# A macaron decoder layer on eight cores: first input in two transfers, norm additions on pairs of blocks, and an instruction order planned with a new DMA model

## The chip, the cores and the metric

The kernel runs on all 8 cores of one Trainium2 chip, one launch, every core with its own share of the data. The time of a run is the device time of the slowest core in microseconds (us). Cores 0 to 3 lie on one die and cores 4 to 7 on the other; "pairs" below are the cores 0 and 1, 2 and 3, 4 and 5, 6 and 7.

Some executions of any kernel here fall into a slower state, in which one or both dies have a lower granted TensorE clock. Such runs are left out of every comparison: 16 of the runs of the changed kernel and of the experiments, and a few of the kernel before. "Fast runs" are the others.

A ratio of two kernels is the mean time of one kernel's fast runs over the mean of the other's fast runs of the same rounds on the same chip, so it is not quite the ratio of the medians that are quoted beside it. The interval behind it is a 95% interval.

## The reference, cut to what matters

One layer; per token the model width is 1024 and the inner width of a feed-forward part (FFN) is 2816. Each core handles one prompt of 2048 tokens with 16 learned tokens ahead of it, and 16 single-token samples: 2080 tokens.

```python
def _rmsnorm(x, g):
    xf = x.astype(jnp.float32)
    y = xf * lax.rsqrt(jnp.mean(xf * xf, axis=-1, keepdims=True) + EPS) * g.astype(jnp.float32)
    return y.astype(x.dtype)

def _swiglu(x, w_gate, w_up, w_down):
    return (jax.nn.silu(x @ w_gate) * (x @ w_up)) @ w_down

def _layer(x, buf_a, buf_b, h0, p):
    x = x + 0.5 * _rmsnorm(_swiglu(_rmsnorm(x, p['g_ffn1_pre']), ...), p['g_ffn1_post'])
    m, nba, nbb, hl = _mixer(_rmsnorm(x, p['g_mix_pre']), buf_a, buf_b, h0, p)   # conv, RG-LRU, gates
    x = x + _rmsnorm(m, p['g_mix_post'])
    x = x + 0.5 * _rmsnorm(_swiglu(_rmsnorm(x, p['g_ffn2_pre']), ...), p['g_ffn2_post'])
    return x, nba, nbb, hl
```

So there are six norms: three before a part ("pre") and three after it ("post"), and each post norm is followed by an addition to x.

## The kernel before

The 2080 tokens lie on the free axis and are cut into five streams of 414 to 418 columns. The model width lies on the partitions in 8 blocks (KC = 8). Streams 0 and 1 form the first group and share each weight as it arrives in fp32 (`wall`, cast to bf16 on the way). The bf16 copy is written back to a scratch buffer (`wsc`), from which streams 2, 3 and 4 read it again, one after the other. Weights come in units of up to 512 KB through a ring of 10 slots (`wring`). Stream 2 joins early: while streams 0 and 1 work through their first FFN, TensorE can also do stream 2's matmuls, because these wait for nothing that streams 0 and 1 produce. I call such matmuls filler.

```python
SIZES = [418, 418, 416, 414, 414]
GROUPS = [[0, 1], [2], [3], [4]]
NW = 10                       # weight slots
XSTEP = [2, 4, 4, 4, 4]       # blocks of x in one transfer, by stream
HEAD = 4
WARM = (44, 12, 10, 10, 40, 50)   # dummy matmuls, meant to keep TensorE's clock up in the head
LAGS = [...]; STARTS = [...]; ENDS = [...]; CLASSES = {...}   # tuned priorities, cut
```

The program records operations with what they read and write; a list scheduler then fixes the order on every engine before anything runs. It plays the operations through a cost model, always takes the one that can start first, and among those within 0.05 us the one with the best tuned priority. On the chip each engine works in this order. An operation whose input is late holds up everything behind it on that engine, even work that is ready.

```python
CAST_BW = 265e3; COPY_BW = 400e3; INPUT_BW = 320e3     # bytes per us
DMA_CAP = (0.72, 0.95); HW_SHARE = (0.43, 0.22)        # when both DMA queues are busy

    def dma(self, eng, fn, reads, writes, nbytes, cast=False, bw=None):
        ...
        o.xfer = nbytes / (bw or (CAST_BW if cast else COPY_BW))
        o.issue = 0.6 if eng == "pool" else 0.1

    def finalize(self):
        ...
        while remaining:
            for e in self.ENGS:
                ...                       # candidates whose inputs and buffers are there
                lo = min(c[0] for c in cands)
                pick = min((c for c in cands if c[0] <= lo + PRI_EPS), key=lambda c: (c[1], c[2]))
            ...
            order[o.eng].append(o)
```

The head: stream 0's x comes in four transfers, the first weight unit and stream 1's x follow on the other queue once the second of them is there, and ScalarE squares stream 0's blocks.

```python
        def issue_unit(g, u):
            S.dma("pool", lambda e: e.dma_start(out=v[0:n](), in_=rows(src, off, n)),
                  [R_xs(STREAMS[0], 3)] if g == 0 else [("wsc", u)], [v, ("wl", g, u)], ...)

        def rms_finish(ps, n):
            rv = newf()
            act(rv[0:n], ps[0:n], AF.Ln, n, [ps] + DP, [rv], bias=EPS, psum=True)   # DP: derived parameters
            act(rv[0:n], rv[0:n], AF.Exp, n, [rv], [rv], scale=-0.5)
            return rv

        def pre_norm(st, gvi, o, halo):
            if st.i <= 1 and gvi == 0:                 # first norm of streams 0 and 1
                for kc in range(KC):
                    sq = newq()
                    act(sq[0:m], xs_view(st, kc, o, n), AF.Square, m, [R_xs(st, kc)], [sq])
                    if st.i == 0 and kc % 2 == 0:
                        keep_warm(WARM[kc // 2])
                    mm_group(ps[0:m], m, [ones[:, :]], [sq[0:m]], ...)     # sum over partitions
            ...                                         # other norms: squares, VectorE sums, one matmul
            rv = rms_finish(ps, m)

        def post_norm(st, acc, o, src32, src_res):
            rv = rms_finish(acc, m)
            for oc in range(KC):
                tv = newf()
                tt(tv[0:m], src32[s][:, oc, 0:m], rv[0:m], ALU.mult, m, src_res(oc, s) + [rv], [tv])
                tt(xs_view(st, oc, o, n), xs_view(st, oc, o, n), tv[0:m], ALU.add, m, ...)

        first(-999.0, load_x, STREAMS[0], "sp", [])
        head = [first(-998.0, issue_unit, 0, 0)]
        first(-997.0, load_x, STREAMS[1], "pool", [R_xs(STREAMS[0], 3)])
```

`final_norm`, the last post norm, is built like `post_norm` and stores two blocks of the output at a time.

## Time and profile before

| | before |
|---|---|
| time, median of 3 runs | 1564.99 us (1564.85 to 1565.97) |
| profiled execution, slowest core (core 0) | 1563.7 us; the 8 cores 1557.1 to 1563.7 us |
| matmuls on each core | 8771 |
| median step from one matmul's start to the next | 0.176 us |
| after the last matmul, mean of 8 cores | 14.3 us |

The page of the profiled execution, core 0. The first line is the busy time of each engine with its share of the span and the number of instructions, the second the chain of work that ended last, by engine.

```profile
...
PE 1532.3 (98%) x8771; PEld 847.6 (54%) x8771; DVE 813.1 (52%) x1535; ACT 771.8 (49%) x1367; POOL 247.7 (16%) x470
...
PE 93%; DVE 3%; DMA 2%; issue 1%; ACT 1%; DVEq 0%; POOL 0%; SPq 0%; ACTq 0%; POOLq 0%
...
```

TensorE is busy 98% of the span. Other engines' work costs time only where TensorE waits for it, so what has to be read is the waits of TensorE. The list of TensorE's waits, core 0 (what it waited for, then us in total, number of times, longest):

```profile
...
engine line waited for: us in total, times, longest us
PE P L662 <- ACT qp L676: 5.9, 5, 3.1
PE P L662 <- DVE qp L680: 3.9, 2, 2.8
PE P L662 <- DVE xs L704: 2.6, 2, 2.2
...
```

These waits are 17 us in all. They understate the loss: after a wait TensorE's clock can fall to one half for a while. The first columns are the stretch and TensorE's busy time with the number of matmuls; near the end of a line stand the granted clock, the DMA share and GB/s.

```profile
...
core 0: us, PE busy (x) PEld busy (x) DVE busy (x) ACT busy (x) POOL busy (x), PEclk, DMA share, GB/s
30.00:100.00 70.00, 67.17 (x371) 36.39 (x370) 22.57 (x40) 19.09 (x35) 3.43 (x7) 0.98 0.85 211
270.00:340.00 70.00, 68.53 (x387) 37.29 (x386) 63.85 (x116) 54.44 (x104) 7.46 (x14) 1.00 0.77 186
1200.00:1260.00 60.00, 57.79 (x319) 31.25 (x318) 47.70 (x119) 36.58 (x64) 11.04 (x21) 0.97 0.54 177
...
```

A full 70 us holds 398 matmuls of 0.176 us. From 30 to 100 us only 371 started, at a clock of 0.98: that is the wait at 77 us with its half-clock stretch. From 1200 to 1260 us it is 319 of 341 possible, for the same reason. A line of the timeline of TensorE on core 0, with the idle time before the instruction in brackets:

```profile
...
80.22 0.34 PE L662 MATMUL P<-qp,ones 128*128 128x416 bf16 x1 [2.83 <-DVE qp L680]
...
```

At 77 us TensorE stood idle for 2.83 us in front of one matmul of stream 2's first norm (416 columns), behind VectorE's sum of the squares for it.

The stretch from 270 to 340 us lies where streams 0 and 1 pass from FFN 1 to the mixer, with four norms on VectorE and ScalarE. The matmuls between 276 and 300 us on core 0, by shape (stream 0's mixer has 402 to 422 columns here, stream 2 has 416):

```profile
...
L662 PE MATMUL P<-hy,wring 128*128 128x416 bf16 x67 | 12.6, 339 | 0.0
L662 PE MATMUL P<-hy,wring 128*128 128x420 bf16 x32 | 6.4, 340 | 0.4 <-ACT fp L676 0.4
L662 PE MATMUL P<-hy,wring 128*128 128x422 bf16 x16 | 3.2, 342 | 0.0
L662 PE MATMUL P<-hy,wring 128*128 128x402 bf16 x16 | 3.0, 332 | 0.0
...
```

Half of this, 67 matmuls or 11.8 us at 0.176 us each, is stream 2's FFN 1, the filler. Stream 1's norm, which these norms end with, comes late and costs little, the timeline of TensorE says:

```profile
...
304.01 0.34 PE L662 MATMUL P<-qp,ones 128*128 128x418 bf16 x1 [1.06 <-DVE qp L680]
...
```

The tail, groups of VectorE instructions after the last projection, core 0 (shape and count, then busy us and mean ns):

```profile
...
L680 DVE TENSOR_TENSOR big<-xs,fp 128x414 f32<-128x414 f32 x8 | 4.7, 591 | 0.8
L680 DVE TENSOR_TENSOR fp<-hy,fp 128x414 f32<-128x414 f32 x8 | 4.7, 584 | 5.0 <-ACT fp L676 5.0
...
```

Sixteen operations of about 0.59 us each, one after the other, with nothing left for TensorE to do.

### The profile page before, as it was taken

To read this page: it belongs to the slowest core of one execution; us is meant where nothing else is said; L and a number is where in the kernel's file an instruction comes from. 1 tells how busy PE (TensorE), PEld (TensorE's weight loads), DVE (VectorE), ACT (ScalarE), POOL (GpSimd) and SP (SyncE) were. 2 spreads that over 40 slices of the span, in tenths; PEclk is the share of its full clock that TensorE was granted. 3 is DMA by queue.
4 is the path that set the end of the run, shared out by engine and by line. 5 is a ranking of instruction groups with operands and counts; after the bars stand their busy time and mean duration, and the time that the engine had idled before them with its cause. 6 is when DMAs were issued, how large, how long until landed. Compare 5 with 4: busy or idle time off the path is not lost.

```text
span 1563.7 us, 27199 instructions; the slowest of 8 cores (1557.1 to 1563.7 us)
## 1 busy us (share of the span) xinstructions
PE 1532.3 (98%) x8771; PEld 847.6 (54%) x8771; DVE 813.1 (52%) x1535; ACT 771.8 (49%) x1367; POOL 247.7 (16%) x470
## 2 busy tenths in 40 slices
PE   8999999999999999999999999999999999999996
PEld 5555555555555555555555555555555555555553
DVE  3232108988787467722127452356567887661143
ACT  3221136788877567411154332446575678451222
POOL 1001111011111111011111122222221111112220
PEclk9999999999999999999999999999999999999998
DMA  9889767766877775898766776655575555545653
GB/s 192 227 193 205 155 159 179 200 146 190 203 162 191 201 201 145 200 203 188 180 178 189 249 247 202 198 181 172 183 254 202 163 174 186 205 170 181 199 185 106
DMA packets 81002, 294.88 MB, mean 189 GB/s; under 512 B 9696, under 2 KB 9824, under 8 KB 80864
## 3 DMA queue, kind: packets, MB, share of 16 engines
q0 software_dynamic: 60704, 223.12, 56.2%
q1 hardware_dynamic: 20160, 70.02, 11.9%
q8 instruction: 74, 1.21, 0.3%
q14 instruction: 64, 0.52, 0.1%
HBM read 284.76 MB, written 64.45 MB: 223 GB/s over the span
## 4 chain that ended last, share of the span: by engine, by line
PE 93%; DVE 3%; DMA 2%; issue 1%; ACT 1%; DVEq 0%; POOL 0%; SPq 0%; ACTq 0%; POOLq 0%
PE P L662 93%; DMA xs<-xin 1%; DMA wring<-wsc 1%; DVE fp L694 1%; DVE fp L680 1%; ACT fp L676 0%; DVE big L680 0%; ACT L676 0%; DVE xs L704 0%; DVE fp L699 0%; DVE fp L688 0%; DVEq L1143 0%; DVE qp L680 0%; ACT qp L676 0%; DVE xs L680 0%
## 5 line engine op out<-in xcount | busy, mean ns | idle before, releaser
L662 PE MATMUL P<-hy,wring 128*128 128x414 bf16 (+4 forms) x6080 | 1101.3, 339 | 5.7 <-DVE xs L704 2.2
L662 PEld LDWEIGHTS P<-hy,wring 128*128 128x128 bf16 x6080 | 591.0, 97 | 487.8 <-issue 14.4
L676 ACT ACTIVATE fp<-P 128x414 f32<-128x414 f32 (+4 forms) x529 | 267.7, 516 | 625.1 <-PE P L662 613.2
L662 PE MATMUL P<-big,wring 128*128 128x414 bf16 (+3 forms) x2400 | 442.8, 338 | 0.3 <-DVE xs L704 0.3
L680 DVE TENSOR_TENSOR big<-P,fp 128x414 bf16<-128x414 f32 (+3 forms) x260 | 151.2, 588 | 403.7 <-PE P L662 379.6
L662 PEld LDWEIGHTS P<-big,wring 128*128 128x128 bf16 x2400 | 233.2, 97 | 189.3 <-issue 1.0
L734 POOL DMA_DIRECT2D wring<-wsc x344 | 182.9, 532 | 802.5 <-PE P L662 786.1
L680 DVE TENSOR_TENSOR fp<-fp 128x414 f32<-128x414 f32 (+3 forms) x215 | 122.5, 572 | 131.2 <-ACT fp L676 124.3
L734 POOL DMA_DIRECT2D wring<-wall x117 | 62.0, 533 | 470.8 <-PE P L662 446.5
L676 ACT ACTIVATE fp<-fp 128x418 f32<-128x418 f32 (+2 forms) x230 | 121.1, 546 | 13.3 <-DVE fp L694 4.0
L676 ACT ACT_TABLE_LOAD x84 | 107.8, 1283 | 28.9 <-PE P L662 19.2
L694 DVE SCALAR_TENSOR_TENSOR fp<-P,par_sb,fp 128x418 f32<-128x418 f32 (+3 forms) x120 | 77.4, 646 | 24.9 <-ACT fp L676 16.9
L694 DVE SCALAR_TENSOR_TENSOR hy<-xs,par_sb,fp 128x414 bf16<-128x414 f32 (+3 forms) x120 | 69.1, 646 | 21.0 <-ACT fp L676 21.0
L694 DVE SCALAR_TENSOR_TENSOR fp<-fp,P 128x414 f32<-128x414 f32 (+3 forms) x80 | 45.4, 580 | 51.6 <-PE P L662 47.5
L676 ACT ACTIVATE fp<-xs 128x414 f32<-128x414 f32 (+3 forms) x104 | 55.1, 545 | 28.2 <-DVE xs L680 27.9
L694 DVE SCALAR_TENSOR_TENSOR fp<-fp,par_sb 128x402 f32<-128x402 f32 (+4 forms) x80 | 51.5, 644 | 7.2
L680 DVE TENSOR_TENSOR fp<-hy,fp 128x414 f32<-128x414 f32 (+3 forms) x80 | 46.7, 584 | 15.6 <-ACT fp L676 15.6
L676 ACT ACTIVATE fp<-fp,dpar 128x418 f32<-128x418 f32 (+2 forms) x80 | 51.1, 639 | 7.2 <-DVE fp L694 1.7
L676 ACT ACTIVATE hy<-P,dpar 128x414 f32<-128x414 f32 (+3 forms) x80 | 48.6, 607 | 7.5 <-ACT fp L676 0.7
L680 DVE TENSOR_TENSOR xs<-xs,fp 128x414 f32<-128x414 f32 (+3 forms) x80 | 47.1, 588 | 6.3 <-DVE fp L680 0.8
L676 ACT ACTIVATE fp<-P,dpar 128x418 f32<-128x418 f32 (+2 forms) x80 | 44.5, 604 | 10.6 <-PE P L662 8.9
L699 DVE TENSOR_TENSOR_SCAN fp<-fp,CAR 128x418 f32<-128x418 f32 (+3 forms) x40 | 43.1, 1076 | 3.8
(44 smaller groups left out, 379.4 us busy)
## 6 DMA issues: line engine op xcount, KB each, us to landing
wring<-wsc POOLq DMA_DIRECT2D x244, 512.0 KB, 4.7
wring<-wall POOLq DMA_DIRECT2D x83, 512.0 KB, 8.2
wsc<-wring SPq DMA_DIRECT2D x83, 512.0 KB, 7.0
wring<-wsc POOLq DMA_DIRECT2D x96, 352.0 KB, 4.1
wring<-wall POOLq DMA_DIRECT2D x32, 352.0 KB, 6.8
wsc<-wring SPq DMA_DIRECT2D x32, 352.0 KB, 5.6
xs<-xin SPq DMA_DIRECT2D x4, 828.0 KB, 7.5
xs<-xin SPq DMA_DIRECT2D x4, 418.0 KB, 6.4
```

What stands on the lines that cost most here:

```text
L662: ins = e.matmul(o, ev(lhs_list[k]), ev(rhs_list[k]), start=(start and k == 0), stop=(stop and k == nk - 1))
L676: return S.op("act", lambda e: e.activation(out=ev(out), in_=ev(in_), func=func, **kw), reads, writes, dur, tbl=TBL.get(func), prio=prio)
L680: return S.op("dve", lambda e: e.tensor_tensor(out=ev(out), in0=ev(in0), in1=ev(in1), op=op), reads, writes, 0.153 + n / 960.0, prio=prio)
L694: return S.op("dve", lambda e: e.scalar_tensor_tensor(out=ev(out), in0=ev(in0), scalar=scalar, in1=ev(in1), op0=op0, op1=op1), reads, writ ...
L699: return S.op("dve", lambda e: e.tensor_tensor_scan(out=ev(out), data0=ev(d0), data1=ev(d1), initial=init, op0=ALU.mult, op1=ALU.add), rea ...
L734: S.dma("pool", lambda e: e.dma_start(out=v[0:n](), in_=rows(src, off, n)), [R_xs(STREAMS[0], 3)] if g == 0 else [("wsc", u)], [v, ("wl", ...
```

## The change

The intent: get the first norm done earlier, shorten VectorE's chains in the norms, and plan the order with a DMA model that describes transfers by packets and by turns between the two queues, so that the plan agrees better with the chip. In pieces:

- Stream 0's x in two transfers; the weights and stream 1's x are released by the first of them. Of every four squares of stream 0's first norm two go to VectorE. A dummy Ln loads ScalarE's table early, and Ln no longer waits for the derived parameters.
- `post_norm` and `final_norm` work on pairs of blocks in place, with the factor `rv` broadcast over the pair.
- New constants for the DMA model, and new tuned priorities. This gives another order on all engines and another choice of slots.
- Dead code (`ACC_TAIL`) goes.

```diff
-XSTEP = [2, 4, 4, 4, 4]
+XSTEP = [4, 4, 4, 4, 4]
 ... LAGS, STARTS, ENDS, CLASSES: all numbers new ...
-CAST_BW = 265e3
-COPY_BW = 400e3
-INPUT_BW = 320e3
-DMA_CAP = (0.72, 0.95)
-HW_SHARE = (0.43, 0.22)
-DMA_LAT = 2.4
+BEGIN = 1.1
+DMA_RATE = 21.5e3
+HW_TURN = 0.82
+DMA_LAT = 2.25
 ...
-        o.xfer = nbytes / (bw or (CAST_BW if cast else COPY_BW))
+        o.xfer = 8 * (nbytes / 128 / DMA_RATE + (stall if stall is not None else 0.085 if cast else 0.055))
 ...
-                c = queues["pool"][0][0].cast
-                return {"pool": DMA_CAP[c] * (1 - HW_SHARE[c]), "sp": DMA_CAP[c] * HW_SHARE[c]}
+                p, h = queues["pool"][0][0].xfer, queues["sp"][0][0].xfer
+                return {"pool": p / (p + HW_TURN * h), "sp": HW_TURN * h / (p + HW_TURN * h)}
 ...
+        act(cst[:, 1:2], cst[:, 0:1], AF.Ln, 1, ["cst"], ["warm"])
 ...
-                  [R_xs(STREAMS[0], 3)] if g == 0 else [("wsc", u)], ...
+                  [R_xs(STREAMS[0], 0)] if g == 0 else [("wsc", u)], ...
 ...
-            act(rv[0:n], ps[0:n], AF.Ln, n, [ps] + DP, [rv], bias=EPS, psum=True)
+            act(rv[0:n], ps[0:n], AF.Ln, n, [ps], [rv], bias=EPS, psum=True)
 ...
-                    act(sq[0:m], xs_view(st, kc, o, n), AF.Square, m, [R_xs(st, kc)], [sq])
+                    if st.i == 0 and kc % 4 > 1:
+                        tt(sq[0:m], xs_view(st, kc, o, n), xs_view(st, kc, o, n), ALU.mult, m, [R_xs(st, kc)], [sq])
+                    else:
+                        act(sq[0:m], xs_view(st, kc, o, n), AF.Square, m, [R_xs(st, kc)], [sq])
 ...
+        def pair(t):
+            return lambda: t().unsqueeze(1).to_broadcast([128, 2, t().shape[-1]])
 ...
         def post_norm(st, acc, o, src32, src_res):
-            for oc in range(KC):
-                tv = newf()
-                tt(tv[0:m], src32[s][:, oc, 0:m], rv[0:m], ALU.mult, m, src_res(oc, s) + [rv], [tv])
-                tt(xs_view(st, oc, o, n), xs_view(st, oc, o, n), tv[0:m], ALU.add, m, ...)
+            xv = XS[s][:, 0:KC * n].rearrange("p (k t) -> p k t", k=KC)
+            for oc in range(0, KC, 2):
+                src, res = src32[s][:, oc:oc + 2, 0:m], src_res(oc, s) + src_res(oc + 1, s)
+                dst, dres = xv[:, oc:oc + 2, o:n], [R_xs(st, oc), R_xs(st, oc + 1)]
+                tt(src, src, pair(rv[0:m]), ALU.mult, 2 * m, res + [rv], res)
+                tt(dst, dst, src, ALU.add, 2 * m, res + dres, dres)
 ... final_norm the same, with the output as destination ...
```

## The prediction

> **What bounds the kernel.** The matmuls. The busy table of the page gives TensorE 98% of the 1563.7 us span; VectorE and ScalarE 52% and 49%. The median step from one matmul's start to the next is 176 ns; 8771 of them make 1544 us. The rest, from the timeline and the list of waits: head (to 29 us), waits in the middle, 14.1 us of tail after the last matmul.
>
> **Head.** Core 0 starts its first projection matmul at 14.7 us; the next ones queue behind stream 1's norm matmul, which waits until 17.4 us for its input (waits of 3.1 and 0.75 us), and the clock falls to one half for 6.8 us. The Trainium skill ("TensorE: Matmul & The Clock Gate", Part 1) gives this gate a half-rate state after an idle window of 3.4 us; this trace agrees, in stretches of 3.4 or 6.8 us. The continuous stream begins at 29.0 us. But the weights limit the head too: units land 3.3 us apart, the third at 25.5 us, and 2.95 us of dummy matmuls stand before it.
>
> **Middle (core 0).** 2.8 us at 77 us (stream 2's norm chain, then 3.4 us at half clock), 1.1 us at 303, 1.0 and 0.9 us for weights at 867 and 1087, 2.2 us at 1231 (small VectorE copies, again half clock), smaller ones later. With the clock about 14 us.
>
> **What the change does.**
> - First input in two transfers, squares split over ScalarE and VectorE. Today the quarters land at 5.1, 7.2, 9.0, 10.1 us; ScalarE's last squares end at 11.2, then Ln waits until 12.62 for the derived parameters, behind the late parameter load. Table load (1.28 us) moves into idle time, Ln no longer waits for parameters. I expect halves at about 7 and 9.7 us, squares done near 10.8, first projection matmul near 13.3: 1.3 us earlier.
> - Norm additions on pairs. One 414-column operation takes 0.588 us, of which 0.157 us is fixed (0.431 us at one column per 1/0.96 ns, the VectorE clock given by the skill's "VectorE: DVE Perf Modes", Specifications). A pair should take 1.02 us. 240 operations become 120: VectorE busy about 813 to 797 us, instructions 1535 to about 1419. On the critical path only in the tail: 16 operations over 9.6 us become 8 over 8.3 us, 1.3 us gained.
> - New order. The new DMA model counts packets and shares turns between the queues. It should keep stream 1's norm matmul from blocking (stream begins at 26 to 27 us), and take away part of the 77, 867 and 1087 us waits; the 1231 us wait has a compute cause and moves unpredictably. Same matmuls, same DMA bytes.
>
> **Sum.** Head 3, tail 1.3, middle 6.5 of 14: about 11 us. Predicted 1554 us, range 1546 to 1563. Faster by over 2% would need under 1533.7 us. Chances: faster 0.01, within 2% 0.98, slower 0.01.
>
> **What would show each step.** Head: timeline, first projection matmul before 14 us, no wait over 2 us behind an input, stream from under 27.5 us. Tail: last matmul to end 12.8 us, pair operations 1.02 us each. Middle: list of TensorE waits summing clearly under today's 17 us, fewer half-clock stretches. VectorE busy near 797 us, TensorE's matmul count 8771.
>
> **What would make it wrong.** The reordered schedule makes new stalls over 3 us, each costing another 1.7 us by the clock; input halves land later than quarters, so the first norm starts later; the broadcast operand makes pair operations slower than 1.02 us; or the head is held by weight arrival alone, so that the earlier first norm buys nothing.

## More of the kernel before

The head, in the chain of work that ended last, core 0, the first 30 us (start, length, what):

```profile
...
8.97 11.87 DMA xs<-xin
...
20.92 0.56 ACT qp L676
...
21.62 8.47 PE P L662 x69
```

The 11.87 us piece is the second half of stream 1's x. Everything of the first norm of stream 0 is missing from this chain.

## The result, and the profile after

| | before | after |
|---|---|---|
| time, median (runs of the first comparison) | 1565.12 us (4 runs) | 1567.10 us (4 runs, one of them slow); the fast ones, with one more, 1563.91, 1564.70, 1565.39 and 1568.81, mean 1565.7 |
| ratio, fast runs | | 1.0003 [0.9985, 1.002]: the same |
| profiled execution, slowest core | 1563.7 us (core 0) | 1563.8 us (core 1) |
| profiled execution, mean of 8 cores | 1561.6 us | 1558.9 us |
| after the last matmul, mean of 8 cores | 14.3 us | 12.9 us |

The predicted 1554 us was about 12 us below the mean of the fast runs, and all of them lie outside the predicted range. The page after, core 1: busy times, the chain, and the group of the new pair operations.

```profile
...
PE 1532.6 (98%) x8771; PEld 848.4 (54%) x8771; DVE 802.7 (51%) x1419; ACT 767.6 (49%) x1365; POOL 247.6 (16%) x470
...
PE 90%; DMA 5%; DVE 2%; ACT 1%; issue 1%; POOL 0%; DVEq 0%; ACTq 0%; POOLq 0%
...
L677 DVE TENSOR_TENSOR hy<-hy,fp 128x828 f32<-128x828 f32 (+3 forms) x40 | 40.7, 1017 | 19.3 <-ACT fp L673 19.3
...
```

VectorE has the predicted 1419 instructions and 802.7 us (predicted 797); a pair takes 1.017 us (predicted 1.02). These pieces did what they should. TensorE's waits, core 1:

```profile
...
engine line waited for: us in total, times, longest us
PE P L659 <- ACT qp L673: 5.1, 4, 1.7
PE P L659 <- DMA wring<-wall: 3.4, 5, 0.9
PE P L659 <- DVE qp L677: 2.7, 1, 2.7
...
```

The sum is 18 us, not less than before, and the names are others. The same three stretches, core 1:

```profile
...
core 1: us, PE busy (x) PEld busy (x) DVE busy (x) ACT busy (x) POOL busy (x), PEclk, DMA share, GB/s
30.00:100.00 70.00, 70.00 (x397) 38.47 (x396) 22.76 (x40) 20.11 (x37) 3.70 (x7) 1.00 0.85 210
270.00:340.00 70.00, 64.45 (x351) 34.20 (x350) 63.46 (x110) 56.15 (x103) 5.82 (x11) 0.95 0.50 135
1200.00:1260.00 60.00, 60.00 (x344) 33.14 (x343) 49.44 (x114) 37.34 (x65) 11.08 (x21) 1.00 0.54 181
...
```

Between 30 and 100 us 397 matmuls started in place of 371, and between 1200 and 1260 us 344 in place of 319: both old waits are gone, about 4.5 us each at 0.176 us per matmul. But between 270 and 340 us it is 351 in place of 387, which gives 6.3 us back, at a clock of 0.95, and the DMA share there fell from 0.77 to 0.50, because weight slots come free only as TensorE goes on. All eight cores show 346 to 351 matmuls there, against 384 to 387 before. The timeline of TensorE in that stretch, core 1 (in runs of several matmuls only one of their shapes is named):

```profile
...
285.69 0.51 PE L659 MATMUL P<-qp,wrgs 128*128 128x418 bf16 x2
287.04 2.97 PE L659 MATMUL P<-hy,wring 128*128 128x416 bf16 x16 [0.84 <-ACT fp L673]
291.08 0.34 PE L659 MATMUL P<-qp,wrgs 128*128 128x418 bf16 x1 [1.07 <-DVE hy L677]
292.35 0.41 PE L659 MATMUL P<-qp,wrgs 128*128 128x418 bf16 x1 [0.93 <-ACT fp L673]
295.48 0.51 PE L659 MATMUL P<-qp,ones 128*128 128x418 bf16 x1 [2.71 <-DVE qp L677]
...
```

After 287 us there are 16 matmuls of stream 2, and then only single matmuls of the mixer's gates and of stream 1's norm, each waiting for its own chain on VectorE and ScalarE. The steps from matmul to matmul at 285.9, 289.7, 291.1 and 292.4 us are 1.17, 1.41, 1.27 and 3.13 us, 6.3 us above the usual 0.176; then the clock is at one half for 6.8 us, which costs 3.4 us more. By shape, core 1 in the corresponding 24 us (it runs about 5 us behind its neighbour):

```profile
...
L659 PE MATMUL P<-hy,wring 128*128 128x416 bf16 x32 | 7.6, 401 | 0.8 <-ACT fp L673 0.8
L659 PE MATMUL P<-hy,wring 128*128 128x420 bf16 x28 | 5.8, 340 | 0.0
L659 PE MATMUL P<-hy,wring 128*128 128x422 bf16 x18 | 4.0, 342 | 0.0
L659 PE MATMUL P<-hy,wring 128*128 128x402 bf16 x8 | 1.5, 332 | 0.0
...
```

The mixer's part is smaller by 10 matmuls and the filler by 35. Part of it was spent earlier: by 270 us core 0 had started 288 of the 352 matmuls of stream 2's gate and up projections, where the old order had started 264. But 64 were left, and only 16 of them ran before the norm. The weights explain that: 16 matmuls use one weight unit, and the queue that loads the units stood still. Core 0, the issues of weight loads for stream 2 (start, length, and the idle time before with its cause):

```profile
...
263.12 0.53 POOL L732 DMA_DIRECT2D wring<-wsc  x1 [4.50 <-PE P L659]
285.28 0.53 POOL L732 DMA_DIRECT2D wring<-wsc  x1 [21.63 <-PE P L659]
...
```

Between the two the queue waited 21.6 us for TensorE to free a slot of the ring; seven loads of new weights (`wall`) had been issued before. The old order issued loads for stream 2 at 274.8, 280.8 and 285.4 us. At the same time the new order wants stream 1's norm sooner, at 290.2 us on core 0 and 295.5 us on core 1 where it was 304.0 us before. In this sequence VectorE had little room: from 262 to 292 us it was busy for 26.9 us on core 0, before 27.1 us. With one unit of filler at hand, TensorE waited.

To see the whole span at once I count, on each core, the matmuls started up to a moment, give each 0.176 us, and subtract that from the moment. The growth of this difference in a stage is the time that the stage lost. (It is negative at first, because the dummy matmuls of the head are shorter.) Both kernels have the same 8771 matmuls, so the sums differ exactly as the spans do. Means of the 8 cores of the profiled executions, in us; the last two columns belong to two experiments below:

| stage | before | after | a_order | b_best |
|---|---|---|---|---|
| to 30 us | −7.8 | −8.8 | −8.7 | −8.1 |
| 30 to 100 | 4.8 | 0.6 | 0.6 | 0.5 |
| 100 to 270 | 1.2 | 1.4 | 1.6 | 1.4 |
| 270 to 340 | 2.4 | 9.0 | 3.0 | 2.3 |
| 340 to 1200 | −0.8 | −0.8 | −0.2 | −0.9 |
| 1200 to 1260 | 3.9 | −0.2 | −0.2 | −0.2 |
| 1260 to the last matmul | −0.1 | 1.1 | 0.8 | −0.3 |
| after the last matmul | 14.3 | 12.9 | 12.9 | 13.7 |
| sum | 17.9 | 15.2 | 9.9 | 8.5 |

So the mean core won 2.7 us, and the new wait took 6.6 of what other stages gave. The slowest core won nothing, because the two cores of a pair drifted apart. The head shows where that begins. The chain in the first 30 us, core 1 and then its neighbour core 0:

```profile
...
8.67 11.68 DMA xs<-xin
...
22.51 11.53 PE P L659 x89
```

```profile
...
8.05 9.32 DMA xs<-xin
...
19.53 14.51 PE P L659 x115
```

On core 1 the second half of stream 1's x takes 11.68 us and TensorE's steady work starts at 22.5 us, about as before (11.87 and 21.6 on core 0 before). On core 0 the same transfer takes 9.32 us. Over the four pairs the second half of stream 1's x landed at 19.5 us on the earlier and 20.6 us on the later core before, and at 17.4 and 20.9 us after. Up to 30 us the earlier core of each pair gained 2.3 us and the later one lost 0.2. The spread of the spans within a pair was 3.1 to 3.5 us in the fast runs of before, and after it 6.4 us in the first comparison and 5.5 us in a_again.

The tail, core 1, as shown of before:

```profile
...
L677 DVE TENSOR_TENSOR big<-xs,hy 128x828 f32<-128x828 f32 x4 | 4.1, 1022 | 0.4
L677 DVE TENSOR_TENSOR hy<-hy,fp 128x828 f32<-128x828 f32 x4 | 4.1, 1017 | 4.0 <-ACT fp L673 4.0
...
```

Eight operations of 1.02 us in place of sixteen of 0.59: 8.2 us in place of 9.4.

### The profile page after: what moved, and what is told of

It reads as the page before. It is cut to its first block, busy times and chain, and to the rows that moved or that the text cites. A ratio compares the mean times of both kernels' runs of the same rounds, so it can differ in the third digit from the quotient of the medians.

```text
span 1563.8 us, 26951 instructions; the slowest of 8 cores (1554.7 to 1563.8 us)
## 1 busy us (share of the span) xinstructions
PE 1532.6 (98%) x8771; PEld 848.4 (54%) x8771; DVE 802.7 (51%) x1419; ACT 767.6 (49%) x1365; POOL 247.6 (16%) x470
## 4 chain that ended last, share of the span: by engine, by line
PE 90%; DMA 5%; DVE 2%; ACT 1%; issue 1%; POOL 0%; DVEq 0%; ACTq 0%; POOLq 0%
PE P L659 90%; DMA wring<-wall 3%; DMA xs<-xin 1%; ACT fp L673 1%; DVE fp L691 1%; DMA wring<-wsc 1%; DVE fp L677 0%; ACT L673 0%; DVE hy L677 0%; DVE big L677 0%; ACT qp L673 0%; DVE xs L701 0%; DVE fp L696 0%; DVE fp L685 0%; DVE xs L677 0%
## 5 line engine op out<-in xcount | busy, mean ns | idle before, releaser
L659 PE MATMUL P<-hy,wring 128*128 128x414 bf16 (+5 forms) x6080 | 1096.2, 338 | 6.0 <-DMA wring<-wall 3.4
L659 PEld LDWEIGHTS P<-hy,wring 128*128 128x128 bf16 x6080 | 589.8, 97 | 487.2 <-issue 13.2
L673 ACT ACT_TABLE_LOAD x85 | 109.1, 1283 | 35.3 <-PE P L659 27.2
L673 ACT ACTIVATE fp<-xs 128x414 f32<-128x414 f32 (+3 forms) x104 | 51.3, 540 | 14.1 <-DVE xs L677 13.3
L677 DVE TENSOR_TENSOR hy<-hy,fp 128x828 f32<-128x828 f32 (+3 forms) x40 | 40.7, 1017 | 19.3 <-ACT fp L673 19.3
L677 DVE TENSOR_TENSOR big<-big,fp 128x414 bf16<-128x414 bf16 (+7 forms) x60 | 42.6, 727 | 12.5 <-ACT fp L673 10.2
L691 DVE SCALAR_TENSOR_TENSOR fp<-fp 128x418 f32<-128x418 f32 (+2 forms) x40 | 23.5, 589 | 44.9 <-ACT fp L673 44.8
```

What stands on the lines that cost most here:

```text
L659: ins = e.matmul(o, ev(lhs_list[k]), ev(rhs_list[k]), start=(start and k == 0), stop=(stop and k == nk - 1))
L673: return S.op("act", lambda e: e.activation(out=ev(out), in_=ev(in_), func=func, **kw), reads, writes, dur, tbl=TBL.get(func), prio=prio)
L677: return S.op("dve", lambda e: e.tensor_tensor(out=ev(out), in0=ev(in0), in1=ev(in1), op=op), reads, writes, 0.153 + n / 960.0, prio=prio)
L691: return S.op("dve", lambda e: e.scalar_tensor_tensor(out=ev(out), in0=ev(in0), scalar=scalar, in1=ev(in1), op0=op0, op1=op1), reads, writ ...
```

## The experiments

Two explanations compete for the wait at 281 to 297 us. Theory O says that the order is to blame: what is left for TensorE at that moment, and what VectorE does first, do not fit each other. The rival P says that the pairs are to blame: an operation of 1.02 us holds up the chain, and lets what follows start only when both blocks are done, so the norm chains there got longer. For the head, the question is whether the first norm or the arrival of data sets the start, and whether the earlier release of the weights is what drives the cores of a pair apart.

Several kernels change one thing but must keep the order, since every edit would give another plan. They build their plan once from the unedited program, then follow its order and its slots while the named part is edited. I call that a frozen order. Their diffs below leave out that machinery.

### a_again: the changed kernel once more, five rounds

No edit.

> The changed kernel once more, beside the others of this call. Expected: same as before within 0.3%. Waits of TensorE between 281 and 297 us on every core (gaps of 1.2, 1.4, 1.3 and 3.1 us between matmul starts) followed by 6.8 us at half clock. One core of each pair (0-1, 2-3, 4-5, 6-7) about 5 us shorter than the other, as in the first runs of it.

Measured: ratio to before 0.9995 [0.9981, 1.001], the fast runs 1565.89, 1565.96 and 1566.23 us, before 1567.13 us (median); the other three runs were slow. The new wait is there again on all cores; the stage from 270 to 340 us lost 9.0 us, as in the first profile. The mean core was 1560.2 us against 1561.9, and the spread within a pair 5.5 against 3.25 us. So the change is worth 1.7 us on the mean core and nothing that can be measured on the slowest.

### a_order: the changed kernel with another order from about 190 to 312 us

```diff
+REORDER = [
+    ("pe", 182, [484, 421, 408, 480, 412, 438, 420, 452]),
+    ("pe", 192, [449, 409, 463, 456, 415, 462, 466]),
+    ...                                     # 30 such stretches on TensorE, ScalarE, VectorE
+]
 ...
+        for e, i, ids in REORDER:
+            assert sorted(o.idx for o in order[e][i:i + len(ids)]) == sorted(ids)
+            order[e][i:i + len(ids)] = [ops[k] for k in ids]
         self.order = order
```

The operations, their slots and the pairs stay; only their sequence on the engines changes. The sequences came from a search with the kernel's own cost arithmetic; whether they are any good only the chip can say.

> The changed kernel with the order of TensorE, ScalarE and VectorE rearranged between about 190 and 312 us and nowhere else: the same operations, buffers and transfers, so that stream 2's independent matmuls are left over for the stretch in which the second norm is awaited. Theory O (the new order spends that filler too early, and this one wait is where the gain of the rest went): the four gaps at 281 to 297 us, 7.0 us in all, shrink to 3.5 us or less, the 6.8 us at half clock after them go or halve, every core is 5 to 8 us shorter (ratio about 0.996). Rival L (the stretch is limited by ScalarE and VectorE whatever the order): the waits come back within the next 40 us and the total changes by under 1 us.

Measured: 1559.95 us (1559.05 to 1561.93), ratio 0.9961 [0.9948, 0.9974] to before; the mean core 1553.7 us. The stretch from 270 to 340 us and the timeline of TensorE in it, core 0:

```profile
...
270.00:340.00 70.00, 68.00 (x384) 37.05 (x383) 61.62 (x113) 60.24 (x112) 7.46 (x14) 1.00 0.64 163
...
```

```profile
...
286.78 12.98 PE L696 MATMUL P<-hy,wring 128*128 128x416 bf16 x72 [0.86 <-DMA wring<-wsc]
...
```

384 matmuls in place of 346 to 351, with the clock at 1.00. 72 matmuls run without a break from 286.8 us, of the mixer and of stream 2. The stage lost 3.0 us in place of 9.0, and all other stages stayed within 0.7 us. Seven cores lost 2.1 to 2.8 us there; on core 6 weights came late (362 matmuls, 6.6 us lost):

```profile
...
293.36 8.95 PE L696 MATMUL P<-hy,wring 128*128 128x416 bf16 x40 [2.10 <-DMA wring<-wsc]
```

Theory O holds: the same operations, pairs included, in another order, are about 6 us faster. This much of the expected gain was lost in this stage.

How the wait went is of interest. a_order did not save up filler: it had started 284 of those 352 matmuls of stream 2 by 270 us, almost as many as the changed kernel. It had more of the rest at hand (36 between 270 and 290 us in place of 16; it issued their weight loads at 271.6 and 283.1 us), and on VectorE it put stream 1's post norm ahead of stream 0's mixer: the last of these pair additions ended at 273.1 us in place of 286.8, and the norm's matmul came at 285.6 us in place of 290.2 (core 0 each). So either side of the gap can be moved, the work that fills it or the chain that ends it. The run does not split the 6 us between the two. What TensorE still waits for on either side of the norm, on core 0 and on core 6, is weights.

### e_single and e_single2: single blocks in post_norm, order frozen

```diff
-                tt(src, src, pair(rv[0:m]), ALU.mult, 2 * m, res + [rv], res)
-                tt(dst, dst, src, ALU.add, 2 * m, res + dres, dres)
+                two(src, src, lambda i, rv=rv: rv[0:m], ALU.mult, 2 * m, res + [rv], res)
+                two(dst, dst, lambda i, src=src: src[:, i, :], ALU.add, 2 * m, res + dres, dres)
```

`two` issues two operations of one block each, as one entry of the plan: they stand one behind the other, and what follows still waits for the second. In e_single the bindings `rv=rv` and `src=src` were missing, so the second operation of each pair read the blocks of the last pair, and its result was wrong. The instructions and their shapes were the right ones, but I had it run again, mended, as e_single2.

> The changed kernel with each pair operation of the two middle norms issued as two operations of one block, one behind the other, in the same place of the same order. Theory O (the order of the work is what makes TensorE wait between 281 and 297 us): gaps there stay, 7.0 us between the four matmul starts becomes 7 to 8 us, total 0 to 1.5 us longer. Rival P (a pair operation of 1.02 us cannot be interrupted and holds up the chain): the four gaps shrink by more than 1 us together, total shorter by 1 us or more.

> As e_single, whose result was wrong by a slip (each second operation read the last pair's blocks), mended: correct, and in time like that run: gaps at 281 to 297 us of 7.0 to 7.6 us in all, 0 to 1.5 us longer than the changed kernel. Under rival P the gaps shrink by more than 1 us.

Measured: e_single 1.0012 [0.9998, 1.0025]; e_single2, correct, 1567.75 us, ratio 1.0009 [0.9996, 1.0022]. The four steps at the wait were 1.18, 1.69, 1.27 and 3.26 us in e_single2 (core 1: in all 7.4 us against 7.0 with pairs), and the stage from 270 to 340 us lost 9.5 us against 9.0. With single blocks the wait is slightly longer, not shorter. So the form of the operation is not the cause. The edit does not test the other half of P, since the chains are still released in pairs. Against that half speaks a_order, which keeps the pairs and loses the wait on seven of eight cores; whether a release after each block would have taken something off the wait in the new order is not shown. That the waits ended with VectorE and ScalarE operations of the norms fits O as well: once nothing else can run, TensorE waits for whatever comes next, and that is a norm.

### t_pairs: the kernel before, with pairs in the last final norm alone

```diff
             events = []
+            if st.last:
+                for oc in range(0, KC, 2):
+                    tt(src, src, <rv broadcast over two blocks>, ALU.mult, 2 * m, res + [rv], res)
+                    tt(ov[:, oc:oc + 2, :], xv[:, oc:oc + 2, o:n], src, ALU.add, 2 * m, ...)
+                    events.append(store_y(st, oc, oc + 2))
+                return events
```

> The kernel before with the last stream's final norm on pairs of blocks and nothing else; its schedule is the same up to there. Expected: last matmul to end 12.8 us instead of 14.2 us on every core, waits elsewhere as before, total 1.3 us shorter (ratio 0.9991). If pair operations were no gain at the end, 14.2 us stays.

Measured: 1565.74 us, ratio 0.9988 [0.9975, 1.0001]; from the last matmul to the end 13.2 us against 14.3 on the mean core, and the mean core's span 1.5 us shorter. The interval just includes 1, so the whole time alone would not show it; the stage does. The pairs in the tail are worth about 1.1 us here (I had expected 1.4) and 1.4 us in the change. In the profiled execution the mean core gained another 1.3 us from 1200 to 1260 us, where nothing was edited: the same step of 2.55 us was followed by the half clock on one core, against seven before. Single executions differ by that much.

### b_squares: the kernel before, with the squares for stream 2's first norm moved up

Four squares on ScalarE, four additions on VectorE and the norm's matmul move ahead of their neighbours; nothing else.

```diff
+REORDER = [
+    ("pe", 97, [104, 293]),
+    ("act", 38, [96, 98, 100, 102, 90, 254, 92, 94, 240, 294]),
+    ("dve", 48, [97, 99, 101, 103, 241]),
+]
```

> The kernel before with four squares of stream 2's first norm moved earlier in ScalarE's order, its four additions one place earlier on VectorE and its matmul one place earlier on TensorE; nothing else. Theory D (the wait at 77 us is there because the old transfer model had the second half of stream 2's input land about 15 us later than the 61 us that the trace shows, so its order holds the squares back): gap of 3.2 us falls under 1 us, no half clock at 80 us, every core 3.5 to 5 us shorter (ratio about 0.997). Rival W (weights limit this stretch): TensorE then waits for weights instead, total within 1 us.

Measured: 1562.2 us, ratio 0.9979 [0.9966, 0.9992]. The step at the wait near 77 us shrank from 3.2 to 1.06 us and the half-clock stretch after it went; the stage from 30 to 100 us lost 1.3 us in place of 4.8. So this wait was the place of nine operations in the order. Stream 2's x had landed at 61.3 us, but in the old order the last four of its squares ran from 76.5 us (core 0), although ScalarE had stood idle for 1.4 and 2.4 us before that. The old plan, played through with the kernel's constants, has this input at 69.4 us, 8 us late and not the 15 us that I had expected; the new plan has it at 60.8 us. So here the new DMA model may cure something, which was not tested apart from the new priorities; but so does the move alone, without the rest of the change.

### b_best: the kernel before, with pairs in the tail and two stretches reordered

The edit of t_pairs, and the same hook as above with sequences for 55 to 110 us and for 1195 to 1250 us.

```diff
+REORDER = [
+    ("pe", 75, [197, 196, 330, 249, 333, 334, 373, 369, 248, 262, ...]),
+    ...
+    ("dve", 1245, [4166, 4192, 4167, 4226]),
+]
```

> The kernel before with pair operations in the last norm, and the order rearranged in two stretches (55 to 110 us, 1195 to 1250 us) so that the waits at 77 and 1231 us should go; head, old transfer model and all the rest as before. If the gains of the change in the middle come from the order of two stretches and the tail alone, this kernel has them without the new stall: 7 to 10 us shorter than before (ratio 0.994 to 0.9955). If they needed the other parts of the change (smaller VectorE load, first norm), under 3 us.

Measured: the fast runs 1555.96 to 1558.42 us, one slow run 1677.69 and one 1782.06; ratio 0.9944 [0.9931, 0.9957], the mean core 1552.8 us, the spread within a pair 3.3 us. Three stretches of the slowest core, core 2:

```profile
...
30.00:100.00 70.00, 70.00 (x398) 38.40 (x396) 22.09 (x40) 20.43 (x38) 4.24 (x8) 1.00 0.93 213
270.00:340.00 70.00, 68.53 (x386) 37.17 (x385) 63.27 (x116) 56.56 (x108) 7.49 (x14) 1.00 0.75 188
1200.00:1260.00 60.00, 60.00 (x344) 33.18 (x342) 51.24 (x133) 40.20 (x72) 11.37 (x22) 1.00 0.54 187
...
```

The first and the last are full now, with 398 and 344 matmuls, and the middle one is as before the change, with 386. This version beats both kernels. It has the old DMA model, the four transfers of the first input, and single blocks everywhere but in the tail. What was good about the change's order can be had from the old order by two local moves, without the new wait.

### c_best: b_best with two more stretches reordered

The hook with further sequences for about 250 to 345 us and 400 to 460 us, and a few swaps later (near 530, 850 and 990 us); otherwise b_best.

```diff
     ("dve", 1245, [4166, 4192, 4167, 4226]),
+    ("pe", 227, [1959, 1958]),
+    ("pe", 229, [1998, 631, 617, 564, 613, 614, 618]),
+    ...
```

> b_best with the order rearranged in two more stretches (250 to 345 us and 400 to 460 us), nothing else. The gaps of 1.4 us at 297 us and 0.7 us at 430 us should shrink; 2 to 4 us shorter than b_best, ratio to before 0.992 to 0.994. If the first part of the kernel is limited by VectorE and ScalarE there, no gain.

Measured: 1556.0 us (1554.57 to 1560.53), ratio 0.9944 [0.9914, 0.9973]; the mean core 1551.4 us, 1.5 us below b_best. The stage from 270 to 340 us lost 1.3 us in place of 2.3. On the slowest core no difference to b_best can be shown; I had expected 2 to 4 us. What is left in these two stages is small.

### h_act: the changed kernel, all squares of the first norm on ScalarE, order frozen

```diff
-                    if st.i == 0 and kc % 4 > 1:
+                    if st.i == 0 and kc % 4 > 1 and not EDIT:
                         tt(sq[0:m], xs_view(st, kc, o, n), xs_view(st, kc, o, n), ALU.mult, m, ...)
```

> The changed kernel with all eight squares of the first norm on ScalarE again, same order and transfers otherwise. Theory A (the head is set by the arrival of the weights, so the quicker first norm buys nothing): the first projection matmul comes 0.7 to 1.5 us later, but the continuous stream begins within 0.5 us of the changed kernel's (about 23 us on the faster core of a pair, 27 us on the slower), total within 1.5 us of it. Rival N (the first norm sets the head): stream and total later by the same 0.7 to 1.5 us on every core.

Measured: 1569.3 us, ratio 1.0025 [0.9997, 1.0053]. The first projection matmul was not later than in the changed kernel (14.6 us on the earlier and 15.6 us on the later core of a pair, against 14.4 and 16.2). The continuous stream of matmuls began at 24.8 and 28.6 us against 24.1 and 28.1. (I count it from the first projection matmul after the last dummy matmuls, as the prediction did with its 29.0 us; the expectations count from a point about 1.3 us earlier.) Squares on two engines bought nothing that can be measured. But that does not show that the norm is unimportant, because the norm did not get slower: on the mean core the squares ended at 12.1 us here and 11.4 us in the change, and Ln, which follows the sum of the squares, began at 13.1 us in both. Between the two lies TensorE, whose order has dummy matmuls between the sums. The changed kernel, core 0, where the last squares were done at 10.7 us:

```profile
...
11.12 0.72 PE L659 MATMUL P<-ones 128*128 128x128 bf16 x10
11.68 0.52 PE L659 MATMUL P<-qp,ones 128*128 128x418 bf16 x2
...
12.29 0.52 ACT L673 ACTIVATE fp<-P 128x418 f32<-128x418 f32 x1 [1.84 <-PE P L659]
```

That the stream waits for stream 1's x and not for this norm rests on the chain shown above.

### h_quarters, h_gate and h_quarters2: who releases the weights, and by how many transfers

Three kernels on the changed one, order frozen. h_quarters brings stream 0's x in four transfers and lets the second release the weights, as before the change. h_gate keeps two transfers and lets the second half release them. h_quarters2 is h_quarters again without a side effect described below.

```diff
-XSTEP = [4, 4, 4, 4, 4]
+XSTEP = [2, 4, 4, 4, 4]                              # h_quarters, h_quarters2
 ...
-                  [R_xs(STREAMS[0], 0)] if g == 0 else [("wsc", u)], ...
+                  [R_xs(STREAMS[0], 3)] if g == 0 else [("wsc", u)], ...      # h_quarters; 7 in h_gate
+                  ["x0gate"] if g == 0 else [("wsc", u)], ...                 # h_quarters2
```

> The changed kernel with its first input in four transfers again (loads behind it released by the second quarter, the same bytes), every engine's order and every buffer as in the changed kernel. Theory H: two large transfers let one core of a pair run ahead (first halves landed at 6.1 us on the winners, 6.9 to 8.3 us on the losers), and it stays ahead. Then the spread inside the pairs falls from about 5.5 us to under 3 us and the slowest core gains 1 to 2 us. Rival: [...]the size of the first transfers does not matter: spread stays at 4 to 6 us, slowest core within 0.5 us. If transfers of a half only delay the norm, squares of the first half start 1 us earlier and nothing else moves.

> The changed kernel with the weights and stream 1's input released by the second half of the first input instead of the first half; same order otherwise. Theory A: every weight lands later by the delay, 1.5 to 3 us, and the stream begins that much later on every core, though the first norm is no later (its second half may even land earlier); total 1 to 3 us longer. Rival S (the early release is what lets one core of a pair run ahead of the other): the two cores of a pair come within 2 us of each other at 30 us, and the slower one is not later than in the changed kernel.

> h_quarters without a side effect that was found in it: its edit had also made 78 later weight loads wait for a later part of stream 0's first middle norm than in the changed kernel. Now only the four transfers differ. Expected at the head as in h_quarters: stream begins near 25 us on the earlier cores of the pairs and 27 us on the later ones (changed kernel: 22.7 and 26.8 us), so the head gain of the earlier cores is gone and the later cores are unchanged. Theory M (the longer total of h_quarters came from the side effect): mean core span 1561 to 1563 us, slowest core within 1.5 us of the changed kernel's, waits for weights after 300 us as in the changed kernel. Rival K (cores of a pair that run in step disturb each other more): total stays 3 us longer than before and pair spread stays above 6 us.

Measured: h_quarters 1569.89 us, ratio 1.002 [1.0007, 1.0033]; h_gate 1586.17 us, ratio 1.0123 [1.0095, 1.0152]; h_quarters2 1566.29 us, ratio 1.0000 [0.9985, 1.0016].

The first two cannot be used as whole times. The name that they wait for, a block of stream 0's x, is written again by the first `post_norm`. With a later block as the gate, 78 weight loads of the first group waited for a later part of that norm. This is my own side effect and has nothing to do with the head; h_quarters2 waits for a name of its own and is free of it.

In the head, h_gate began its stream of matmuls at 28.4 and 29.9 us (earlier and later core of a pair), later than the change on both (24.1 and 28.1). So releasing the weights at the first half is right, and it is not what makes the later core late; but with the later release the two cores start 1.5 us apart in place of 4.1, as that rival expected. h_quarters2 began at 25.9 and 27.4 us. Halves in place of quarters help the earlier core of a pair by about 2 us and the later one not at all. On the whole time quarters and halves are the same: the mean core 1560.0 us and the slowest 1563.8 us in h_quarters2's fast runs.

One thing stays open. The spread within a pair is 5.4 us in h_quarters2 too, although its head starts the cores only 1.5 us apart, so theory H, that the two large transfers make the spread, falls. So part of the drift arises later, while weights stream. TensorE's waits for weight DMAs between 40 us and the end were 0.5 to 1.2 us on the earlier cores and 1.9 to 5.1 us on the later ones of the changed kernel, 2.4 to 8.4 us in a_order, 0 to 3.2 us in b_best, and 0.2 to 2.7 us before. That the two cores of a pair take from each other is a guess that fits; none of these runs separates it from the new order's timing of weights.

## Why the prediction was right or wrong

The prediction subtracted three terms: head 3 us, tail 1.3 us, middle 6.5 us.

- **Tail, right.** Predicted 1.3 us; measured 1.4 us (14.3 to 12.9 us) in the change, 1.1 us in t_pairs alone. The cost of a pair was worked out from one 0.588 us operation with a fixed part of 0.157 us and one column per cycle of VectorE's 0.96 GHz, which the Trainium skill gives ("VectorE: DVE Perf Modes", Specifications). The trace agrees: 1.017 us for 828 columns, with the broadcast operand.
- **VectorE's totals, right.** 1419 instructions as predicted and 802.7 us against 797. Off the critical path this was worth nothing, as said.
- **Head, wrong.** "It should keep stream 1's norm matmul from blocking (stream begins at 26 to 27 us)" and the earlier first norm were to give 3 us. The mean core got 1.0, the earlier core of each pair 2.3, the later one −0.2, and the slowest core decides. Three steps failed. The first norm did not come earlier: the squares were done at 11.4 us (predicted 10.8), but their sum stood behind dummy matmuls on TensorE, so that the first projection matmul came at 15.3 us on the mean core, predicted 13.3 and before 15.1. The 3 us were counted from core 0, where the stream began at 29.0 us, the latest of the eight; their mean was 27.2 us before and 26.1 us after. And the stream does not wait for this norm. The prediction named a risk of this kind ("the head is held by weight arrival alone, so that the earlier first norm buys nothing") and then did not follow it up in the trace. The chain of work before already says it: first x, then 11.87 us of stream 1's x, which shares the queue with the weights, then TensorE.
- **Middle, wrong; this is the step that failed.** "take away part of the 77, 867 and 1087 us waits" and half of the 14 us of waits was the term of 6.5 us. The waits at 77 and 1231 us did go, and more fully than expected: 4.2 and 4.1 us on the mean core. From 340 to 1200 us the two weight waits went and others came (on core 1 near 549, 603 and 770 us); the stage lost the same. But the new order made a wait that the old one did not have, 6.6 us from 270 to 340 us, and 1.2 us after 1260 us. The sum of the middle is 0.2 us in place of 6.5. This was the first item under "what would make it wrong": "The reordered schedule makes new stalls over 3 us, each costing another 1.7 us by the clock". The clock's part was 3.4 us. What failed is the subtraction: it counted the waits that would go, and none that another order would bring.
- **Where the gain went.** a_order takes the new wait away on seven of eight cores, changes little else, and is 0.9961 of before, 1560 us: about half of the way from the measured time to the predicted 1554 us. Of the rest about 2 us lie between the cores of a pair: against before in the same rounds a_order's mean core is 7.5 us shorter (1553.7 us) and its slowest 5.6 us (1558.7 against 1564.2 us). The remaining 3 to 4 us no core had on the mean, above all 2 of the 3 us of the head.

I had taken a better DMA model to mean a better order. The three waits that mattered, at 77, 1231 and 285 us, are waits of TensorE for VectorE and ScalarE. In the first the old plan had a landing 8 us late; that the other two came from the place of compute operations is shown for both by reordering alone (b_best, a_order). The scheduler's own plan, played through with the kernel's constants, is arithmetic and no measurement, but it already contains waits of 8.4 us between 281 and 297 us, where the old plan has 2.0; the old plan has 5.1 us from 40 to 100 and 1.9 us from 1200 to 1260 us, where the new one has none. Its total, 1549.0 us, is not shorter than that of the old kernel's plan, 1548.3 us. A look at both would have shifted the prediction.

The half clock: the Trainium skill ("TensorE: Matmul & The Clock Gate", Part 1) says that TensorE falls to half rate after an idle window of about 3.4 us. The trace agrees in the size of the stretches, 3.4 or 6.8 us, but not in the condition: the longest step here was 3.13 us, and near 1231 us a single step of 2.55 us was enough on seven of eight cores before, on five in b_squares and on one in t_pairs. So the half clock after such a step is partly chance, and 1.7 us of a core's time with it.

## What to carry to other kernels

When one engine is at 98% and everything runs in a planned order, new tuned priorities are the largest part of a change, whatever the diff says about its other parts. Compare the two orders where the dependent chains are (here norms) and ask what independent work is left for the bound engine at that moment, which chain the other engines finish first, and whether the weights of that work have a slot by then: work that is spent early, or has no weights, cannot fill a gap. Ahead of the first full stretch of matmuls, follow the chain of arrivals on the slower core of each pair before counting a faster first operation as a gain, and count lost matmuls by stage, core by core, since a gain on the cores that end early does not shorten the kernel.

## What the Trainium skill lacked or had wrong

- "TensorE: Matmul & The Clock Gate", Part 1, advises to budget 1.95 GHz (13/16) for dense matmuls on all cores under the default power profile, as a state that holds while the load lasts. Here eight cores ran dense matmuls for 1.5 ms at a granted clock of 0.99 and 0.176 us per matmul of 418 columns, in most runs. A clock of 0.83 to 0.84 was seen only in the slow runs, on one die in one (1838.79 us). Which power profile the chip ran under is not on record.
- The same part gives an idle window of about 3.4 us as the condition for half rate. The runs show 6.8 us of half clock after four gaps of 1.2, 1.4, 1.3 and 3.1 us with short work between them, and 3.4 us after a single step of 3.2 us near 77 us or of 2.55 us near 1231 us, but not on every core. The part also tells of a kernel in which frequent short idles between groups of matmuls did it, but it does not say how much work within a window keeps the clock.
- "HBM Reference" gives both cores of a domain the same share of bandwidth when both stream, about 358 GB/s. The runs show the cores of a pair below that and unequal in the head: from 8 to 20 us of the changed kernel core 0 moved 237 GB/s and core 1 216, the same transfer took 9.32 us on core 0 and 11.68 us on core 1, and over four pairs it landed at 17.4 and 20.9 us. No page says that two cores with the same program drift apart; either core can lead (core 0 in the first profile, core 1 in that of a_again).
- "Vector Engine (DVE) Microarchitecture Reference" says which performance mode an operation takes when one input repeats a row, but gives no duration for it. The runs show, in fp32, 1.017 us for 828 columns with the factor repeated over two blocks, against 1.022 us for the addition of 828 columns without repeat, so the repeat cost nothing that can be seen.
